# A hybrid diffusion step on one core: the low half of the attention scores with 16-bit operands

## The chip, the cores and the metric

One core of a Trainium2 chip. The metric is the time in microseconds (us) of one execution on the device. TensorE (PE in the profile) multiplies, VectorE (DVE), ScalarE (ACT) and GpSimd (POOL) do the rest, and all DMAs are issued by SyncE (SP).

## What is computed

Two layers over 256 context tokens (the prompt) and 2048 latent tokens (the samples), width 1024. A layer normalises and modulates its input, projects it to 2816 columns, runs attention (8 query heads, 2 key and value heads of 64), a short convolution and a pooling side by side, and projects back. The part that matters here:

```python
q = _rmsnorm(q.reshape(B, n, N_HEADS, HEAD_DIM), q_g)
k = _rmsnorm(k.reshape(B, n, N_KV_HEADS, HEAD_DIM), k_g)
...
s = jnp.einsum('bqkgd,btkd->bkgqt', qblk, k).astype(jnp.float32) * scale
p = jax.nn.softmax(s, axis=-1)
return jnp.einsum('bkgqt,btkd->bqkgd', p.astype(v.dtype), v)
```

The samples attend to 2048 rotated keys of their own and 256 cached ones, the prompt to its own 256.

## The kernel before

[...] To keep accuracy, an operand x is split into a high part h (x rounded to F32R) and a low part l = x - h, and a product is made of several: h*h, l*h and h*l.

**Two phases per layer.** Phase A (`phase_a`) projects: for each 256 columns of the input weights it multiplies all blocks of tokens (L473 to L475, L631 to L633; about 48 products to a unit), splits what it has, transposes q and k to head-major form and stores everything in scratch DRAM. A unit of q (`q_unit`, L531) leaves its result in one of five PSUM buffers; ACT copies it out (L487), DVE and POOL rotate it, and some units later `post` (L540) transposes it on PE (L544), copies the high part on ACT (L550), subtracts on DVE (L551) and hands two halves of each to `store`. Stores are kept back by one hook and then issued on SP, in order (`stores`, L171). The tiles of this work come from a ring of nine buffers, `w2`. `put_k` (L572) does the same for k.

Phase B (`phase_b`) is attention and the output projection. A unit is one head with 512 queries: 9 steps of 256 keys each, 32 units for the samples in a layer and 4 short ones for the prompt. `load_q1` (L1076) fills T1 with q's high and low part in the two halves of the partitions, KH holds k's high part twice, and so one product of 128 rows gives (qh + ql)*kh. `load_q2` (L1083) fills T2: 64 rows of qh and a 65th row, the shift. KL holds k's low part in 64 rows and ones in the 65th. A step (`qk`, L1151) makes for each of two key tiles

```python
nc.tensor.matmul(out=ps[:, i, :], lhsT=u.KH[u.g][:, kt], rhs=u.T1, start=True, stop=False)
nc.tensor.matmul(out=ps[:, i, :], lhsT=u.KL[u.g][0:65, kt], rhs=u.T2, start=False, stop=True)
```

The shift is minus the maximum over the keys plus a constant, so that the exponential stays in range. It is found ahead of the unit by products of their own (`max_pieces`, L1116 and L1123) with a DVE maximum after each (L1117, L1125), spread by `max_a` and `max_b` (L1143), whose last instruction writes it to T2's 65th row on ACT (L1146). After `qk` ACT takes the exponential twice, as F32 (L1165) and as F32R (L1167), POOL subtracts the two into a 16-bit low part (L180), DVE sums (L1187), and `pv` multiplies by v: the F32R part with V (L1201), and the 16-bit part with VH, a 16-bit copy of v's high half, in two column halves side by side (L1208). `round_v` (L1039) makes VH on ACT (L1041). The output projection of the block before is laid between the steps (L1328 to L1330).

The order of PE's work is written out by hand: a loop over steps calls pieces of the maximum, `qk`, `pv` three steps behind, and the output projection, at places fixed by the table `PR`. `load_kv` (L1026) loads k and v of one group; the tiles are made by `kv_tiles` (L1008). At the end of phase B `half` (L1415) loads output weights into tiles that k and v no longer need.

Of the kernel before, what the change touches and what calls it, by code (L numbers as in the profile page):

```python
# [9 lines left out]
F32 = mybir.dt.float32  # L10
# [13 lines left out]
NP = 256  # L24
# [15 lines left out]
V_SCALE = 0.0625  # L40

# [54 lines left out]
def hybrid_step(ctx: ExitStack, tc: tile.TileContext, A, O):  # L96
# [24 lines left out]
    qL = [scratch(f"qL{p}", [128, NS], F32) for p in range(4)]  # L121
    qHp = [scratch(f"qHp{p}", [128, NP], F32) for p in range(4)]
    qLp = [scratch(f"qLp{p}", [128, NP], F32) for p in range(4)]
    kH = scratch("kH", [128, NS + NC], F32)
    kL = scratch("kL", [128, NS + NC], F32)
    kHp = scratch("kHp", [128, NP], F32)
    kLp = scratch("kLp", [128, NP], F32)
# [39 lines left out]
    def store(out, in_):  # L167

        late[1].append((out, in_.bitcast(F32)))
# [18 lines left out]
    def setup(tp, ptr):  # L188
# [13 lines left out]
        nc.vector.memset(lift, P_LOG2 * float(np.log(2.0)) * 8.0)  # L202
# [63 lines left out]
    def phase_a(l, xs_src, xp_src, nxt):  # L266


        with ExitStack() as st, ExitStack() as left:
# [261 lines left out]
            def q_unit(w, b, pair, c):  # L531
# [8 lines left out]
                def post(pair, q):  # L540
# [10 lines left out]
                    nc.vector.tensor_tensor(out=lv, in0=tr, in1=hv, op=ALU.subtract)  # L551
                    t0 = b.t0 + pair * 256
                    for hp in range(2):
                        dh, dl = (qHp, qLp) if b.prompt else (qH, qL)
                        store(dh[2 * c + hp][:, t0:t0 + 256], hv[:, hp, :])
                        store(dl[2 * c + hp][:, t0:t0 + 256], lv[:, hp, :])
# [15 lines left out]
            def put_k(k, dh, dl):  # L572
# [4 lines left out]
                lo = w1("kl", F32R)  # L577
                nc.scalar.copy(out=h[:, 0:256], in_=tr)
                nc.vector.tensor_tensor(out=lo[:, 0:256], in0=tr, in1=h[:, 0:256], op=ALU.subtract)
                store(dh, h[:, 0:256])  # L580
                store(dl, lo[:, 0:256])
# [415 lines left out]
    def phase_b(l, xs_src, xp_src, xs_dst, xp_dst, nxt):  # L997
# [3 lines left out]
        with ExitStack() as st, ExitStack() as left:  # L1001
# [6 lines left out]
            def kv_tiles(prompt):  # L1008
                if prompt:
                    t = wk.tile([128, 4, 512], F32R, tag="cl", name="kvp", bufs=1)  # L1010
                    vh = wk.tile([128, 2, 2, 64], F16, tag="VHp", name="VHp", bufs=1)
                    for g in range(2):
                        for a, v in zip(kvs[True], (t[:, g, 0:256], t[:, g, 256:512],
# [6 lines left out]
                for a, t in zip(kvs[False], (p.tile([128, n], F32R, tag=f"KH{g}", name="KH"),  # L1020
                                             p.tile([65, n], F32R, tag=f"KL{g}", name="KL"),
                                             p.tile([128, n // 128, 128], F32R, tag=f"V{g}", name="V"),
                                             p.tile([128, n // 128, 64], F16, tag=f"VH{g}", name="VH"))):
                    a.append(t)

            def load_kv(prompt, g, first=True, second=True):  # L1026
# [7 lines left out]
                if second:  # L1034
                    load(KL[g][0:64, 0:n], sl[r, :])
                    nc.vector.tensor_copy(out=KL[g][64:65, 0:n], in_=ones1[64:65, 0:1].to_broadcast([1, n]))
# [46 lines left out]
            def load_q2(u):  # L1083
                sh = qHp if u.prompt else qH
                u.T2 = lk.tile([65, 512], F32R, tag="T2", name="T2", bufs=3)
                for r, ts, c in q_parts(u):
                    load(u.T2[0:64, c], sh[u.pair][r, ts])
# [625 lines left out]
```

## Time and profile before

| | us |
|---|---|
| median of 3 runs | 3377.59 |
| lowest, highest | 3371.95, 3385.19 |
| the profiled execution | 3372.27 |
| its span, first to last instruction | 3370.4 |
| PE busy | 3185.3 |
| DVE, POOL, ACT busy | 2442.1, 2136.2, 1833.3 |

The mean granted clock of TensorE is 0.98 of full speed. The first layer's phase A lasts to about 700 us, its phase B to 1690, the second layer's phases to 2345 and 3370. In the profile, L12 is line 12 of the kernel. Matmul records overlap, and their ends are modelled: the time that one of a row of them takes is read from start to start. PEld is the loading of weights, which runs beside PE.

### The profile page before, as it was taken

The page shows a single profiled execution, that of the slowest core. Times are in us where ns is not written, and L with a number is a line of the kernel's source. Part 1 is how long each engine was busy: PE and PEld are TensorE (multiplying, and loading weights), DVE is VectorE, ACT ScalarE, POOL GpSimd, SP SyncE. Part 2 cuts the span into 40 slices and gives each one's busy share as a digit, 9 for nine tenths or more (in the row PEclk, how much of TensorE's full clock was granted, in tenths as well). Part 3 has the DMA queues.
Part 4 walks back from the last instruction along what each step waited for, and adds up shares of the span by engine and source line. Part 5 has one row for each costly group of instructions (what it writes and reads, how often), then busy time and mean ns, then how long its engine had stood idle before and what let it go on. Part 6 is the DMA issues. An engine that isn't in the chain of part 4 may idle for free. (4 is left out here: it accounts for less than half of the span.)

```text
span 3370.4 us, 48172 instructions
## 1 busy us (share of the span) xinstructions
PE 3185.3 (95%) x17818; PEld 2517.4 (75%) x17818; DVE 2442.1 (72%) x3860; ACT 1833.3 (54%) x2618; POOL 2136.2 (63%) x1192
## 2 busy tenths in 40 slices
PE   6899999988999999999999999999899999999998
PEld 5888788765677777777789787987567676776777
DVE  5645575368888888888568546735888988998886
ACT  3222332248777777777543323323877677776773
POOL 3324352248888898888644345422888888888884
PEclk9999999999999999999999999999999999999999
DMA  7256635441241323232643564435123424233245
GB/s 240 72 157 204 218 125 167 135 113 34 82 147 51 101 75 93 59 101 83 203 147 98 172 197 145 128 100 128 51 66 104 133 62 126 67 110 105 74 142 197
DMA packets 367010, 405.26 MB, mean 120 GB/s; under 512 B 20788, under 2 KB 314680, under 8 KB 366008
## 3 DMA queue, kind: packets, MB, share of 16 engines
q1 hardware_dynamic: 366776, 402.18, 38.6%
q8 instruction: 142, 2.33, 0.3%
q14 instruction: 92, 0.75, 0.1%
HBM read 284.12 MB, written 117.98 MB: 119 GB/s over the span
## 5 line engine op out<-in xcount | busy, mean ns | idle before, releaser
L180 POOL TENSOR_TENSOR pl<-P,ph 128x1024 f16<-128x1024 f32 (+2 forms) x594 | 1407.6, 2379 | 328.8 <-ACT ph L1167 305.5
L1165 ACT ACTIVATE P<-st 128x1024 f32<-128x1024 f32 x576 | 635.9, 1104 | 436.7 <-PE st L1156 426.4
L1117 DVE TENSOR_REDUCE mr<-mx 128x1 f32<-128x512 f32 x1024 | 693.7, 684 | 232.5 <-PE mx L1116 230.2
L1187 DVE TENSOR_REDUCE Z<-P 128x152 f32<-128x912 f32 (+2 forms) x576 | 695.8, 1208 | 7.0 <-ACT P L1165 6.0
L1167 ACT ACTIVATE ph<-st 128x1024 fp32r<-128x1024 f32 x584 | 591.0, 1012 | 0.0
L631 PE MATMUL rest<-xh,wh 128*128 128x512 f32 (+1 forms) x1280 | 486.1, 380 | 0.3 <-ACT wh L424 0.3
L1116 PE MATMUL mx<-KH,T 128*128 128x512 f32 x1024 | 451.1, 441 | 37.1 <-DVE mr L1117 30.9
L633 PE MATMUL rest<-xh,wl 128*128 128x512 f32 (+1 forms) x1280 | 476.1, 372 | 5.2 <-DVE wl L426 3.4
L632 PE MATMUL rest<-xl,wh 128*128 128x512 f32 (+1 forms) x1280 | 476.5, 372 | 0.9 <-POOL xl L180 0.9
L1155 PE MATMUL st<-T,KH 128*128 128x512 f32 x1152 | 462.5, 402 | 1.4 <-ACT ph L1167 1.4
L1156 PE MATMUL st<-T,KL 65*128 65x512 f32 x1152 | 462.8, 402 | 0.0
L1201 PE MATMUL pv<-ph,V 128*128 128x512 f32 x1152 | 373.7, 406 | 10.1 <-DVE o L1220 10.1
L1116 PEld LDWEIGHTS mx<-KH,T 128*128 128x128 f32 x1024 | 196.4, 192 | 196.2 <-DVE mr L1117 92.8
L633 PEld LDWEIGHTS rest<-xh,wl 128*128 128x128 f32 x1280 | 243.7, 190 | 48.8 <-DVE wl L426 4.0
L426 POOL TENSOR_TENSOR wl<-wf,wh 128x512 fp32r<-128x512 f32 x88 | 123.8, 1407 | 244.3 <-ACT wh L424 229.0
L631 PEld LDWEIGHTS rest<-xh,wh 128*128 128x128 f32 x1280 | 244.3, 191 | 45.7 <-issue 7.1
L632 PEld LDWEIGHTS rest<-xl,wh 128*128 128x128 f32 x1280 | 244.3, 191 | 38.5 <-POOL xl L180 1.2
L1156 PEld LDWEIGHTS st<-T,KL 65*128 65x128 f32 x1152 | 220.9, 192 | 48.0
L1155 PEld LDWEIGHTS st<-T,KH 128*128 128x128 f32 x1152 | 221.2, 192 | 39.8 <-issue 4.2
L474 PE MATMUL qkv<-wl,xh 128*128 128x256 f32 x864 | 246.1, 285 | 4.1 <-DVE wl L426 2.9
L473 PE MATMUL qkv<-wh,xh 128*128 128x256 f32 x864 | 249.7, 289 | 0.0
L475 PE MATMUL qkv<-wh,xl 128*128 128x256 f32 x864 | 245.6, 284 | 0.0
(230 smaller groups left out, 5816.6 us busy)
## 6 DMA issues: line engine op xcount, KB each, us to landing
wo<-woH SPq DMA_DIRECT2D x68, 512.0 KB
wo<-woL SPq DMA_DIRECT2D x68, 512.0 KB
wf<-in_w_in SPq DMA_DIRECT2D x50, 512.0 KB
wa<-in_w_ada SPq DMA_DIRECT2D x24, 1024.0 KB
wf<-in_w_in SPq DMA_DIRECT2D x19, 1024.0 KB
woH<-wgh SPq DMA_DIRECT2D x64, 256.0 KB
woL<-wgl SPq DMA_DIRECT2D x64, 256.0 KB
T<-qH SPq DMA_DIRECT2D x128, 128.0 KB
```

What stands on the lines that cost most here:

```text
L180: nc.gpsimd.tensor_tensor(out=out, in0=a, in1=b, op=op)
L631: nc.tensor.matmul(out=ps[:, 0:b.n], lhsT=wh[:, k, ms], rhs=b.h[:, k, :], start=(k == 0), stop=False)
L632: nc.tensor.matmul(out=ps[:, 0:b.n], lhsT=wh[:, k, ms], rhs=b.l[:, k, :], start=False, stop=False)
L633: nc.tensor.matmul(out=ps[:, 0:b.n], lhsT=wl[:, k, ms], rhs=b.h[:, k, :], start=False, stop=(k == KD - 1))
L1116: nc.tensor.matmul(out=ps, lhsT=u.T1[:, q * 128:(q + 1) * 128], rhs=u.KH[u.g][:, c * 512:(c + 1) * 512])
L1117: nc.vector.reduce_max(out=mr[:, q, c:c + 1], in_=ps, axis=AX.X)
L1155: nc.tensor.matmul(out=ps[:, i, :], lhsT=u.KH[u.g][:, kt], rhs=u.T1, start=True, stop=False)
L1156: nc.tensor.matmul(out=ps[:, i, :], lhsT=u.KL[u.g][0:65, kt], rhs=u.T2, start=False, stop=True)
L1165: nc.scalar.activation(out=P, in_=ps, func=AF.Exp, scale=0.125)
L1167: nc.scalar.activation(out=ph, in_=ps, func=AF.Exp, scale=0.125)
L1187: nc.vector.tensor_reduce(out=z[:, c], in_=u.P[grp][:, 0:ns, c, :].rearrange("p s n t -> p n s t"), axis=AX.XY, op=ALU.add)
L1201: nc.tensor.matmul(out=u.po, lhsT=u.V[u.g][:, 2 * j + i, :], rhs=ph[:, i, :], start=(j == 0 and i == 0), stop=False)
```

## The change

T2 becomes a 16-bit float tile and is loaded from a new scratch copy of q, `qB`, in 16 bits; `post` makes this copy with one more ACT instruction and stores it. KL becomes 16-bit from `put_k` on: the subtraction writes 16 bits, the scratch tensor and its loads halve. Since the shift doesn't fit the format's steps as it is, it is stored divided by 256 (`M_SCALE`; ACT's scale and the constant `lift`), and KL's row of ones becomes a row of 256, written by a memset. KL and VH of a group become two parts of one tile, `L0` or `L1`, and the tile that takes over KL1's place at the end takes L1's.

```diff
--- before.py
+++ after.py
@@ -38,6 +38,7 @@
       'n2': 4, 'fh': 0, 'tpos': 0, 'ze': 0, 'ds': 1, 'zb': 3, 'dl': 2, 'm3': 1000, 'hk': 2, 'hc': 2,
       'fd': 12, 'n1': 9, 'h0': 22, 'h1': 16, 'h2': 10, 'fl': 2, 'dc': 256, 'el': 5, 'mapos': 1}
 V_SCALE = 0.0625
+M_SCALE = 256.0
 
 
 C_Q, C_K, C_V, C_ZA = 0, 512, 640, 768
@@ -119,12 +120,14 @@
 
     qH = [scratch(f"qH{p}", [128, NS], F32) for p in range(4)]
     qL = [scratch(f"qL{p}", [128, NS], F32) for p in range(4)]
+    qB = [scratch(f"qB{p}", [128, NS], F16) for p in range(4)]
     qHp = [scratch(f"qHp{p}", [128, NP], F32) for p in range(4)]
     qLp = [scratch(f"qLp{p}", [128, NP], F32) for p in range(4)]
+    qBp = [scratch(f"qBp{p}", [128, NP], F16) for p in range(4)]
     kH = scratch("kH", [128, NS + NC], F32)
-    kL = scratch("kL", [128, NS + NC], F32)
+    kL = scratch("kL", [128, NS + NC], F16)
     kHp = scratch("kHp", [128, NP], F32)
-    kLp = scratch("kLp", [128, NP], F32)
+    kLp = scratch("kLp", [128, NP], F16)
     vS = scratch("vS", [128, 18, 2, 128], F32)
     vSp = scratch("vSp", [128, 2, 2, 128], F32)
     zS = [scratch(f"zS{p}", [128, NS], F32) for p in range(4)]
@@ -166,7 +169,7 @@
 
     def store(out, in_):
 
-        late[1].append((out, in_.bitcast(F32)))
+        late[1].append((out, in_ if in_.dtype == F16 else in_.bitcast(F32)))
 
     def stores():
         for out, in_ in late[0]:
@@ -199,7 +202,7 @@
         nc.vector.memset(ones1, 1.0)
         nc.vector.memset(vones, V_SCALE)
         nc.vector.memset(vones_h, V_SCALE)
-        nc.vector.memset(lift, P_LOG2 * float(np.log(2.0)) * 8.0)
+        nc.vector.memset(lift, P_LOG2 * float(np.log(2.0)) * 8.0 / M_SCALE)
         nc.vector.memset(sT, 0.0)
         nc.vector.tensor_copy(out=ones_r, in_=ones1[:, 0:1].to_broadcast([128, 128]))
         pr = ptr.tile([128, 100], F32, tag="tr", name="pr")
@@ -549,9 +552,12 @@
                     lv = lo.rearrange("p (a n) -> p a n", a=2)
                     nc.scalar.copy(out=hv, in_=tr)
                     nc.vector.tensor_tensor(out=lv, in0=tr, in1=hv, op=ALU.subtract)
+                    qb = w2("qb").bitcast(F16)[:, 0:512].rearrange("p (a n) -> p a n", a=2)
+                    nc.scalar.copy(out=qb, in_=tr)
                     t0 = b.t0 + pair * 256
                     for hp in range(2):
-                        dh, dl = (qHp, qLp) if b.prompt else (qH, qL)
+                        dh, dl, db = (qHp, qLp, qBp) if b.prompt else (qH, qL, qB)
+                        store(db[2 * c + hp][:, t0:t0 + 256], qb[:, hp, :])
                         store(dh[2 * c + hp][:, t0:t0 + 256], hv[:, hp, :])
                         store(dl[2 * c + hp][:, t0:t0 + 256], lv[:, hp, :])
 
@@ -574,11 +580,11 @@
                 for i in range(2):
                     nc.tensor.transpose(tr[:, i * 128:(i + 1) * 128], k[:, i * 128:(i + 1) * 128], ident)
                 h = w1("kh", F32R)
-                lo = w1("kl", F32R)
+                lo = w1("kl").bitcast(F16)[:, 0:256]
                 nc.scalar.copy(out=h[:, 0:256], in_=tr)
-                nc.vector.tensor_tensor(out=lo[:, 0:256], in0=tr, in1=h[:, 0:256], op=ALU.subtract)
+                nc.vector.tensor_tensor(out=lo, in0=tr, in1=h[:, 0:256], op=ALU.subtract)
                 store(dh, h[:, 0:256])
-                store(dl, lo[:, 0:256])
+                store(dl, lo)
 
             def kv_unit(w, b, pair):
                 ps = qkv_mm(w, b, pair)
@@ -1010,17 +1016,17 @@
                     t = wk.tile([128, 4, 512], F32R, tag="cl", name="kvp", bufs=1)
                     vh = wk.tile([128, 2, 2, 64], F16, tag="VHp", name="VHp", bufs=1)
                     for g in range(2):
-                        for a, v in zip(kvs[True], (t[:, g, 0:256], t[:, g, 256:512],
+                        for a, v in zip(kvs[True], (t[:, g, 0:256], t[0:65, g, 256:384].bitcast(F16),
                                                     t[:, 2 + g, 0:256].rearrange("p (t e) -> p t e", e=128), vh[:, g])):
                             a.append(v)
                     return
                 n = NS + NC
                 g = len(kvs[False][0])
                 p = kvp if g else lk
-                for a, t in zip(kvs[False], (p.tile([128, n], F32R, tag=f"KH{g}", name="KH"),
-                                             p.tile([65, n], F32R, tag=f"KL{g}", name="KL"),
+                low = p.tile([128, n + n // 2], F16, tag=f"L{g}", name="L")
+                for a, t in zip(kvs[False], (p.tile([128, n], F32R, tag=f"KH{g}", name="KH"), low[0:65, 0:n],
                                              p.tile([128, n // 128, 128], F32R, tag=f"V{g}", name="V"),
-                                             p.tile([128, n // 128, 64], F16, tag=f"VH{g}", name="VH"))):
+                                             low[:, n:].rearrange("p (t e) -> p t e", e=64))):
                     a.append(t)
 
             def load_kv(prompt, g, first=True, second=True):
@@ -1032,8 +1038,8 @@
                     for i in range(2):
                         load(KH[g][64 * i:64 * i + 64, 0:n], sh[r, :])
                 if second:
-                    load(KL[g][0:64, 0:n], sl[r, :])
-                    nc.vector.tensor_copy(out=KL[g][64:65, 0:n], in_=ones1[64:65, 0:1].to_broadcast([1, n]))
+                    nc.sync.dma_start(out=KL[g][0:64, 0:n], in_=sl[r, :])
+                    nc.vector.memset(KL[g][64:65, 0:n], M_SCALE)
                     load(V[g], sv[:, :, g, :])
 
             def round_v(prompt, g):
@@ -1081,10 +1087,10 @@
                     load(u.T1[u.lo, c], sl[u.pair][r, ts])
 
             def load_q2(u):
-                sh = qHp if u.prompt else qH
-                u.T2 = lk.tile([65, 512], F32R, tag="T2", name="T2", bufs=3)
+                sb = qBp if u.prompt else qB
+                u.T2 = lk.tile([65, 512], F16, tag="T2", name="T2", bufs=3)
                 for r, ts, c in q_parts(u):
-                    load(u.T2[0:64, c], sh[u.pair][r, ts])
+                    nc.sync.dma_start(out=u.T2[0:64, c], in_=sb[u.pair][r, ts])
 
             def load_z(u):
                 z = wk.tile([128, 512], F32, tag="zs", name="zs", bufs=2)
@@ -1143,7 +1149,8 @@
             def max_b(u):
                 ps = borrow["ps"]() if borrow else pmx.tile([128, 512], F32, tag="mx", name="mxb")
                 nc.tensor.matmul(out=ps, lhsT=ones_r, rhs=u.dg)
-                nc.scalar.activation(out=u.T2[64:65, :], in_=ps[64:65, :], func=AF.Identity, bias=lift[64:65, :])
+                nc.scalar.activation(out=u.T2[64:65, :], in_=ps[64:65, :], func=AF.Identity, bias=lift[64:65, :],
+                                     scale=1.0 / M_SCALE)
 
 
             GRP = 3
@@ -1413,7 +1420,7 @@
                         state["ss"] = sm.tile([128, 4, 4], F32, tag="oss", name="oss", bufs=1)
 
                 def half(i):
-                    load_w(i // 2, i % 2, kvp.tile([128, KD, 256], F32R, tag=("KH1", "KL1", "V1")[i], name="wt"), 0)
+                    load_w(i // 2, i % 2, kvp.tile([128, KD, 256], F32R, tag=("KH1", "L1", "V1")[i], name="wt"), 0)
 
                 def later():
                     load_w(2, 1, wk.tile([128, KD, 256], F32R, tag="P", name="wt", bufs=2), 0)
```

## Rows read from the trace of the kernel before

**Rows 1.** Busy time of each engine in five stretches (start:end, length, then engines).

```profile
core 0: us, PE busy (x) PEld busy (x) DVE busy (x) ACT busy (x) POOL busy (x), PEclk, DMA share, GB/s
0.00:700.00 700.00, 648.15 (x3932) 548.52 (x3933) 388.65 (x808) 203.23 (x375) 243.96 (x207) 0.97 0.52 163
700.00:1690.00 990.00, 948.31 (x5046) 704.10 (x5045) 800.30 (x1078) 701.93 (x878) 815.24 (x385) 0.98 0.32 96
1690.00:2345.00 655.00, 626.23 (x3712) 551.25 (x3711) 384.95 (x738) 208.13 (x382) 253.91 (x209) 0.99 0.43 136
2345.00:3290.00 945.00, 897.03 (x4647) 654.06 (x4645) 820.75 (x1114) 696.80 (x947) 791.66 (x365) 0.97 0.32 96
```

**Rows 2.** The page's chain of work that ended last, shares of the span.

```profile
PE 28%; DVE 7%; DMA 2%; ACT 2%; issue 1%; POOL 1%; SPq 0%; POOLq 0%; ACTq 0%; DVEq 0%
PE mx L1116 3%; PE pv L1201 3%; PE st L1155 3%; PE st L1156 3%; PE pv L1208 2%; PE rest L633 2%; PE rest L631 2%; PE rest L632 2%; DVE mr L1117 2%; DVE Z L1187 2%; PE op L1328 1%; PE op L1329 1%; PE op L1330 1%; DMA wo<-woL 1%; PE lc L1235 1%
```

**Rows 3.** The same chain within 2345 to 3290 us, by line.

```profile
by line: PE mx L1116 11.7%; PE pv L1201 10.6%; PE st L1156 9.8%; PE st L1155 9.8%; PE pv L1208 6.5%; DVE mr L1117 6.2%; DVE Z L1187 5.4%; PE op L1328 4.6%; PE op L1329 4.5%; PE op L1330 4.4%; DMA wo<-woL 3.0%; issue 2.6%; PE lc L1235 2.5%; 
```

**Rows 4.** PE in order of time, 1009.4 to 1011.8 us: start, length, line, tiles, count.

```profile
1009.41 0.63 PE L1201 MATMUL pv<-ph,V 128*128 128x512 f32 x2
1009.98 0.62 PE L1208 MATMUL pv<-pl,VH 128*64 128x512 f16 x4
1010.53 0.50 PE L1116 MATMUL mx<-KH,T 128*128 128x512 f32 x1
1010.86 0.40 PE L1155 MATMUL st<-T,KH 128*128 128x512 f32 x1
1011.10 0.39 PE L1156 MATMUL st<-T,KL 65*128 65x512 f32 x1
1011.33 0.40 PE L1155 MATMUL st<-T,KH 128*128 128x512 f32 x1
1011.56 0.40 PE L1156 MATMUL st<-T,KL 65*128 65x512 f32 x1
1011.80 0.40 PE L1116 MATMUL mx<-KH,T 128*128 128x512 f32 x1
```

**Rows 5.** All instructions of line L1156: duration ns min/median/max, first and last start.

```profile
L1156 PE MATMUL st<-T,KL x1152: 389/399/632, 712.6 to 3305.2; 65*128 65x512 f32 x192
...
L1156 PE MATMUL st<-T,kvp x16: 393/400/628, 743.4 to 2464.8; 65*128 65x512 f32 x16
```

**Rows 6.** Durations of L1208 (1010.2 to 1010.5 us) and of L1156 (1005 to 1030 us).

```profile
L1208 PE MATMUL pv<-pl,VH x4: 379/391/403, 1010.0 to 1010.2; 128*64 128x512 f16 x4
...
L1156 PE MATMUL st<-T,KL x18: 394/396/403, 1004.6 to 1028.8; 65*128 65x512 f32 x18
```

**Rows 7.** PE in order of time around a column-tiled 32-bit product, first projection stage.

```profile
218.40 0.39 PE L631 MATMUL rest<-xh,wh 128*128 128x512 f32 x1
218.63 0.39 PE L632 MATMUL rest<-xl,wh 128*128 128x512 f32 x1
218.86 0.39 PE L633 MATMUL rest<-xh,wl 128*128 128x512 f32 x1
219.17 1.07 PE L228 MATMUL aps<-wa,sT 128*32 128x256 f32 x16
220.18 0.50 PE L631 MATMUL rest<-xh,wh 128*128 128x512 f32 x1
```

**Rows 8.** Waits, whole span: engine, line, released by, us in total, times, longest.

```profile
ACT P L1165 <- PE st L1156: 426.4, 387, 5.4
...
DVE mr L1117 <- PE mx L1116: 230.2, 343, 4.6
...
PEld mx L1116 <- DVE mr L1117: 92.8, 186, 3.3
...
PE mx L1116 <- DVE mr L1117: 30.9, 45, 3.0
...
ACT raw L487 <- DMA qH<-qh: 14.3, 3, 6.1
```

**Rows 9.** Instructions on the tile qh: SP stores, ACT copy, DVE subtraction.

```profile
L173 SPq DMA_DIRECT2D qH<-qh x64: 319/423/3204, 106.8 to 2170.4; - x64
L550 ACT CAST qh<-trq x36: 565/568/592, 104.9 to 2168.2; 128x512 fp32r<-128x512 f32 x36
L551 DVE TENSOR_TENSOR ql<-trq,qh x36: 675/684/693, 105.6 to 2169.4; 128x512 fp32r<-128x512 f32 x36
```

**Rows 10.** Busy time of each engine in stretches of the projection stages.

```profile
480.00:600.00 120.00, 119.04 (x778) 103.91 (x778) 70.78 (x183) 35.34 (x66) 38.27 (x33) 0.99 0.47 141
1790.00:1850.00 60.00, 59.23 (x490) 58.69 (x490) 47.24 (x135) 19.31 (x39) 22.45 (x21) 1.00 0.43 135
```

**Rows 11.** Groups of the constant and shift rows, and DMA issues with KB each.

```profile
L1036 DVE CAST KL<-ones 1x2304 fp32r<-1x2304 f32 x4 | 7.8, 1959 | 6.5 <-DMA mL<-ml 6.4
...
L1146 ACT ACTIVATE T<-mxb,lift 1x512 fp32r<-1x512 f32 x70 | 47.5, 679 | 2.8 <-PE mxb L1145 1.1
...
T<-qH SPq DMA_DIRECT2D x128, 128.0 KB
...
KL<-kL SPq DMA_DIRECT2D x4, 576.0 KB
```

## Prediction

> **What bounds the kernel now.** Read the stages first [rows 1]. The two attention stages (700 to 1690 and 2345 to 3290 us) take 1935 us. In them PE is busy 96% and 95% of the time; the next engines are DVE (81%, 87%) and POOL (82%, 84%). In the two projection stages PE is busy 93% and 96% and ACT only 29% to 32%. A busy PE is not PE at its peak, since matmuls overlap, so the chain of work that ended last is read next [rows 2]: it reaches back over 41% of the span, and PE holds 28 of those 41 points, DVE 7. In the second attention stage alone, the line to be changed (L1156, the second score product) is 9.8% of the window, as much as its partner L1155 [rows 3]. So the chain runs through the changed instruction, though not at all times.
>
> Then one step of the loop, in order of time [rows 4]. From 1010.86 to 1011.80 us four score products start 0.23 to 0.24 us apart, with nothing between: a 32-bit product of 512 columns occupies PE for 0.94 / 4 = 0.235 us. Everything below hangs on that spacing. The weight load of each product begins as its predecessor starts and is over before the predecessor is, so a shorter load buys nothing.
>
> **The change part by part.**
>
> *The second score product with 16-bit operands.* There are 1152 + 16 = 1168 of them [rows 5]. The kernel has 16-bit products already: the low part of PV, L1208, column-tiled in pairs. Its records fall into two lengths [rows 6]: 403 ns for the first pair of a group, which carries the exposed weight load, and 379 ns for the second. The 32-bit products of the same stretch have 394 to 403, median 396. That is 17 ns shorter, but ends are modelled, so I check it by starts. The group of four begins at 1009.98 and lasts 0.62 us, so its last pair starts at 1009.98 + 0.62 - 0.38 = 1010.22; the next product starts at 1010.53, 0.31 later [rows 4]. This contains the change of tiling, whose price a purely 32-bit place shows: L633 to the column-tiled L228 is 219.17 - 218.86 = 0.31, against 0.23 from one L631 to L633 product to the next [rows 7], so 0.08 to 0.09 us. What is left for the 16-bit product is 0.22 us, against 0.235. I take 17 ns: 1168 x 17 ns = **19.9 us less on PE**. Bounds: nothing (lengths and starts are uncertain by about as much), and, if the following 32-bit product gained as much, 40 us.
>
> *How much of this reaches the end.* In the second layer 584 of the products occupy 584 x 0.235 = 137 us, and the chain holds 9.8% of 945 = 93 us of them [rows 3], 68%. The rest lies beside DVE: PE's loads of the maximum product waited 92.8 us for DVE's maxima, and PE itself 30.9 us [rows 8]; there a faster PE only waits longer. 19.9 x 0.68 = **13.5 us**. If all landed, 20 us.
>
> *Changing type between neighbours.* Each 16-bit product now stands between 32-bit ones, so PE changes type 2336 times. The trace shows such a change only together with one of tiling. It costs the same there (the second L1201 starts at 1009.41 + 0.63 - 0.40 = 1009.64, L1208 at 1009.98: 0.34 less 0.235, so 0.1) as the change of tiling between 32-bit products [rows 4, 7]. I therefore take 0 for the type. The upper bound is a whole visit to L1208: from 1009.64 to the product at 1010.86 is 1.22 us for four products' worth of time, 0.94, so 0.28 us. The changed product keeps 65 rows and 128 columns, so it is not tiled.
>
> *The copy of q.* Each of 36 head transposes gets one more ACT copy, priced like the existing one at 568 ns, 36 x 0.57 = 20.5 us, and two more stores (72 SP issues of about 0.42 us, 30 us of SP) [rows 9]. All of it lies in the projection stages. In the two stretches chosen there PE is busy 99%, ACT 29% and 32% [rows 10]: PE hides it. Without that cover it is 20.5 us, and 36 x 0.68 = 24.6 more if the ACT copy has to follow DVE's subtraction out of the same bank: 45 us. The third buffer per transpose turns the ring of nine work buffers faster; waits on it exist (ACT raw for the store of qh: 14.3 us in 3 times [rows 8]) and may double, but five PSUM buffers stand between ACT and PE. I take 1 us. What is queued behind the copy on ACT (raw copies, weight casts) moves by half a microsecond. On SP the new stores go ahead of those of qh and ql; their waits were there before.
>
> *Small edits.* The 64 loads of T2 for the sample rows halve from 128 KB, the four of KL from 576 KB [rows 11]; the attention stages have DMA at 0.32 [rows 1], so nothing. The constant row of KL becomes a memset in place of a cast that cost 1.96 us four times [rows 11]: between 0 and -8 us of DVE, 0 taken. The ACT write of the shift row keeps its shape, 679 ns [rows 11]; the scale rides along. KL and VH share one tile; VH's four casts come where they came before.
>
> **Sum.** 0 - 13.5 + 1 = -12.5 us. The profiled execution took 3372.3 us (span 3370.4), 5.3 below the median of the runs shown, so against the median 3377.6 I forecast **3365 us**, 0.4% less. A measurement of this kernel tells about 0.5%, 17 us, from no change.
>
> **Rivals.**
>
> 1. *More lands than the chain says.* Where PE waits for DVE, DVE had often waited for PE (230.2 us for the maximum product, ACT 426.4 us for the score product [rows 8]), so a faster PE pulls both forward. 20 us and up to the 40 of the upper bound: about 3357, at best 3340. For it: no other engine is above 87% busy. Against it: the waits above.
>
> 2. *The width buys nothing.* If the 0.235 us is the price of 512 columns whatever their type, PE gains 0, and time is 3378 + 1, say 3379. The recorded 379 against 396 speaks against it; that these ends are modelled, and that the starts leave 0.22 with an uncertainty of 0.01, speaks for it. [...]
>
> 3. *Slower, by the change of type.* The place is PE between L1155 and L1156, twice for each product. If a change of type makes PE empty itself, it costs up to 0.28 us for each visit: 1168 x 0.28 = 327 us, of which the chain's 68% is 222: 3600, with half the price 3489. It turns into a loss as soon as a visit costs over 17 ns. For it: every 16-bit group of the trace has a gap on both sides. Against it: the same gap stands between 32-bit products where the tiling changes [rows 7].
>
> 4. *Slower, by the projection stages.* The extra copy and the ring make ACT late in freeing PSUM, and the 45 us above come onto the path: 3378 - 13 + 45 = 3410. It would need ACT to fall behind by five units of qkv products; ACT has two thirds of its time free.
>
> That the program would not do what it says (the product still run as 32-bit) is not a live case, since both operands are declared 16-bit and loaded so.
>
> **How the numbers follow.** Forecast (13.5 us land, give or take 6): 0.50, split evenly on both sides of the 17 us, since a median moves by some microseconds too. Rival 1: 0.16, faster. Rival 2: 0.19, of which 0.18 the same and 0.01 slower. Rival 3: 0.10, slower. Rival 4: 0.05, slower. Faster 0.25 + 0.16 = 0.41; same 0.25 + 0.18 = 0.43; slower 0.01 + 0.10 + 0.05 = 0.16. The range reaches down to rival 1's best case and up past rival 2 by the scatter of the runs (8 us from the median to the highest) and a few microseconds of the ring: 3340 to 3392. Rivals 3 and 4 (0.15) are left out, and a little of the edges. The forecast's own range is 3352 to 3376.
>
> **What the profile of after would show.** Right: L1156 with 16-bit forms, records near 380 ns and 0.215 to 0.22 us to the next start, L1155 unchanged at 0.235; four score products in 0.90 to 0.91 us instead of 0.94; PE's wait for DVE's maxima some microseconds up; the projection stages as long as before to within 2 us, with 36 more ACT copies. Wrong: a gap on PE before or after L1156 (rival 3); unchanged 0.235 (rival 2); a projection stage longer by over 10 us, with ACT raw or the store of the copy as releaser (rival 4); attention stages shorter by 20 us or more together (rival 1).

## The result and the profile after

| us | before | after |
|---|---|---|
| median | 3375.47 | 3399.94 |
| lowest, highest | 3370.47, 3385.19 | 3394.21, 3403.39 |
| span of the profiled execution | 3370.4 | 3399.2 |

The ratio is 1.0068, with a 95% interval from 1.0052 to 1.0083: the change makes the kernel slower by 24 us, where 12 us faster was forecast, and the time lies above the range.

To find the stage that pays, cut both executions at the same work and not at the same times: at the first and the last KH product (the line of [rows 4] that starts a step) of each layer. First the busy time of each engine in the four stretches of the kernel after (start:end, length, then engines).

```profile
core 0: us, PE busy (x) PEld busy (x) DVE busy (x) ACT busy (x) POOL busy (x), PEclk, DMA share, GB/s
0.00:719.30 719.30, 663.50 (x3985) 560.55 (x3986) 390.71 (x817) 214.63 (x397) 243.18 (x207) 0.97 0.51 161
719.30:1657.50 938.20, 902.72 (x4744) 567.16 (x4743) 780.28 (x1054) 690.68 (x860) 804.19 (x377) 0.98 0.29 86
1657.50:2356.90 699.40, 662.53 (x3936) 585.66 (x3935) 384.44 (x747) 218.11 (x402) 257.38 (x216) 0.97 0.45 143
2356.90:3333.90 977.00, 921.43 (x4745) 577.98 (x4743) 834.18 (x1137) 715.08 (x972) 807.01 (x377) 0.97 0.31 94
```

The same cuts in the kernel before.

```profile
0.00:712.40 712.40, 660.55 (x3986) 558.55 (x3987) 394.94 (x818) 205.20 (x380) 243.96 (x207) 0.97 0.51 161
712.40:1655.40 943.00, 904.47 (x4745) 664.45 (x4744) 782.13 (x1054) 691.21 (x860) 805.93 (x378) 0.98 0.30 89
1655.40:2334.70 679.30, 651.53 (x3934) 576.88 (x3933) 392.74 (x747) 208.46 (x383) 258.44 (x215) 0.99 0.46 145
2334.70:3305.00 970.30, 916.77 (x4744) 667.82 (x4743) 835.47 (x1138) 715.42 (x972) 808.17 (x378) 0.98 0.32 97
```

The number of PE instructions is the same to within two, so the lengths can be compared. The projection stages grew by 6.9 and 20.1 us, 27 together. The attention stages, where the gain should be, went by -4.8 and +6.7. (That makes 28.8 us between the two executions; the profiled one of before lies 3 us under the median above, that of after 1 us over its own.) In the second projection stage PE's idle time (length less busy) rose from 27.8 to 36.9 us, and its busy time rose by 11 us for the same products. The granted clock beside it fell from 0.99 to 0.97, which over 680 us is 13.6 us by these rounded figures, an estimate. So the loss there has two halves: PE waits longer, and it runs slower.

Who waits for whom stands in the waits of the kernel after (engine, line, released by, us in total, times, longest).

```profile
ACT P L1172 <- PE st L1163: 431.9, 385, 5.1
PEld L1163 <- issue: 306.2, 1163, 0.5
POOL wl L429 <- ACT wh L427: 299.6, 57, 18.6
DVE mr L1123 <- PE mx L1122: 227.4, 339, 4.5
...
ACT qb L556 <- DVE ql L554: 132.1, 31, 10.0
...
ACT raw L490 <- PE qkv L478: 44.8, 11, 7.2
```

The rows of attention (ACT P, DVE mr) answer to [rows 8] and hardly moved. Two lines are new. ACT's copy of q waits 132.1 us for DVE's subtraction, 31 times out of 36. And the weight load of the changed product starts late 1163 times out of 1168, by 0.26 us each time, "issue": nothing that the profile shows holds it. Two old lines moved; in the waits of the kernel before they read

```profile
POOL wl L426 <- ACT wh L424: 229.0, 47, 19.2
...
ACT raw L487 <- PE qkv L475: 112.1, 26, 9.0
```

POOL waits 299.6 us for ACT's weight casts, 229.0 before. And ACT waits for PE's qkv products only 44.8 us in 11 times, 112.1 us in 26 times before: that line was ACT's slack (the time by which it is ahead of its supplier), and more than half of it is spent.

Here is one of the 31. ACT in order of time in the kernel after (in brackets the idle time before, and what ended it).

```profile
1822.92 0.58 ACT L553 CAST qh<-trq 128x512 fp32r<-128x512 f32 x1 [1.85 <-POOL ra L183]
1831.19 0.58 ACT L556 CAST qb<-trq 128x512 f16<-128x512 f32 x1 [7.69 <-DVE ql L554]
1831.67 0.59 ACT L490 COPY raw<-qkv 128x512 f32<-128x512 f32 x1
...
1838.03 0.58 ACT L556 CAST qb<-trq 128x512 f16<-128x512 f32 x1 [4.57 <-DVE ql L554]
```

DVE in the same stretch.

```profile
1822.43 3.36 DVE L516 TENSOR_TENSOR sq<-raw,trig 128x128 f32<-128x128 f32 x4
1825.72 0.16 DVE L156 TENSOR_SCALAR nt_v<-hs 128x16 f32<-128x16 f32 x1
...
1829.26 1.29 DVE L525 TENSOR_TENSOR ra<-ra,nt_y 128x512 f32<-128x512 f32 x2
1830.47 0.68 DVE L554 TENSOR_TENSOR ql<-trq,qh 128x512 fp32r<-128x512 f32 x1
```

ACT is ready for the copy at 1823.5. DVE has the subtraction in its queue behind a rotation and a whole chain of small normalisation steps and gets to it at 1830.47. Both only read the transposed q, the one PSUM tile `trq`. The copy starts at 1831.19, when the subtraction is over (1830.47 and 0.68 us), and for 7.69 us the raw copies and weight casts behind it on ACT stand still. So one reader waits here for the other, 31 times; what makes it wait the trace doesn't show. Three of PE's own waits in the second projection stage, kernel after, show where this reaches it:

```profile
PE qkv L476 <- ACT wh L427: 3.2, 1, 3.2
...
PE trq L547 <- ACT qb L556: 1.7, 1, 1.7
...
PE rest L637 <- ACT wh L427: 1.7, 1, 1.7
```

In the same stage of the kernel before, the first two aren't there and the third is 0.3 us. They are a weight cast that stands on ACT behind the copy, and a PSUM buffer of the transposes that the copy still reads. In neither kernel does a qkv product wait for ACT's raw copy: their five PSUM buffers never ran out. And over the stretch that the prediction had picked as the proof of its cover [rows 10], kernel after:

```profile
1790.00:1850.00 60.00, 54.82 (x457) 54.21 (x456) 40.87 (x126) 19.65 (x38) 18.70 (x16) 1.00 0.43 133
```

PE is busy 54.82 us of 60, with 457 products, where it had 59.23 and 490 (the kernel after began this stage 2 us later). ACT is busy 19.65 us, as before (19.31): its share never showed the danger.

The second new line, on PE. A step of the kernel after, PE in order of time.

```profile
1018.82 0.39 PE L1162 MATMUL st<-T,KH 128*128 128x512 f32 x1
1019.05 0.39 PE L1163 MATMUL st<-T,L 65*128 65x512 f16 x1
1019.09 0.59 PE L1162 MATMUL st<-T,KH 128*128 128x512 f32 x1
1019.52 0.39 PE L1163 MATMUL st<-T,L 65*128 65x512 f16 x1
```

The weight loads of the same step.

```profile
1018.59 0.19 PEld L1162 LDWEIGHTS st<-T,KH 128*128 128x128 f32 x1
1019.04 0.10 PEld L1163 LDWEIGHTS <-L 65*128 65x128 f16 x1 [0.26 <-issue]
1019.05 0.20 PEld L1162 LDWEIGHTS st<-T,KH 128*128 128x128 f32 x1
1019.51 0.10 PEld L1163 LDWEIGHTS <-L 65*128 65x128 f16 x1 [0.26 <-issue]
```

Don't read single gaps here: a 32-bit product behind a 16-bit one has its start recorded 0.04 us after it, and a record of 0.59 us. Read pairs: from one L1163 to the next it is 0.47 us here, as for a pair of 32-bit products; the median of all such pairs at full clock is 0.461 us, against 0.469 in the kernel before. The load of the 16-bit weights takes half the time (0.10 against 0.19 us), but it begins 0.22 us after the 32-bit product before it has started, about when that has streamed, and not as it starts.

### The profile page after: what moved, and what is told of

Read it like the earlier page. It is cut to its first block, busy times and chain, and to the rows that moved or that the text cites. A ratio compares the mean times of both kernels' runs of the same rounds, so it can differ in the third digit from the quotient of the medians.

```text
span 3399.2 us, 48325 instructions
## 1 busy us (share of the span) xinstructions
PE 3203.6 (94%) x17818; PEld 2342.1 (69%) x17818; DVE 2426.7 (71%) x3860; ACT 1851.6 (54%) x2654; POOL 2131.6 (63%) x1192
## 5 line engine op out<-in xcount | busy, mean ns | idle before, releaser
L1122 PE MATMUL mx<-KH,T 128*128 128x512 f32 x1024 | 528.4, 517 | 36.5 <-DVE mr L1123 28.5
L1162 PE MATMUL st<-T,KH 128*128 128x512 f32 x1152 | 505.1, 497 | 1.5 <-ACT ph L1174 1.5
L1163 PE MATMUL st<-T,L 65*128 65x512 f16 x1152 | 458.5, 398 | 0.0
L1208 PE MATMUL pv<-ph,V 128*128 128x512 f32 x1152 | 386.1, 417 | 10.2 <-DVE o L1227 10.2
L1163 PEld LDWEIGHTS <-L 65*128 65x128 f16 x1152 | 113.5, 99 | 300.8 <-issue 300.1
L429 POOL TENSOR_TENSOR wl<-wf,wh 128x512 fp32r<-128x512 f32 x88 | 121.7, 1384 | 299.6 <-ACT wh L427 299.6
L1162 PEld LDWEIGHTS st<-T,KH 128*128 128x128 f32 x1152 | 229.9, 200 | 13.4 <-issue 4.2
```

The costliest lines, as they stand in the source:

```text
L1122: nc.tensor.matmul(out=ps, lhsT=u.T1[:, q * 128:(q + 1) * 128], rhs=u.KH[u.g][:, c * 512:(c + 1) * 512])
L1208: nc.tensor.matmul(out=u.po, lhsT=u.V[u.g][:, 2 * j + i, :], rhs=ph[:, i, :], start=(j == 0 and i == 0), stop=False)
```

## The experiments

Three theories for the loss: **Theory 1**, ACT's wait for DVE in the projection stages; **Theory 2**, the change of type on PE; **Theory 3**, the ring of work buffers and the 72 more stores. Later, on the size of the gain: **Theory A**, a 16-bit weight load isn't taken ahead behind a 32-bit product but is behind a 16-bit one; **Theory B**, it is never taken ahead. "Stage" below is a stretch between the cuts of the section above; each ratio is to runs of the kernel before on the same chip.

**The copy ahead of the subtraction** (the kernel after, two lines moved)

```diff
                     nc.scalar.copy(out=hv, in_=tr)
+                    qb = w2("qb").bitcast(F16)[:, 0:512].rearrange("p (a n) -> p a n", a=2)
+                    nc.scalar.copy(out=qb, in_=tr)
                     nc.vector.tensor_tensor(out=lv, in0=tr, in1=hv, op=ALU.subtract)
-                    qb = w2("qb").bitcast(F16)[:, 0:512].rearrange("p (a n) -> p a n", a=2)
-                    nc.scalar.copy(out=qb, in_=tr)
```

> The changed kernel with the 16-bit copy of q issued on ACT ahead of DVE's subtraction out of the same bank, so that ACT no longer waits for DVE there. Theory 1 (the loss is ACT's wait for DVE's subtraction, 132.1 us in 31 times, which holds up the projection stages): back to the time of before or a little under it, 3365 to 3380, both projection stages within 4 us of before. Theory 2 (the loss is the change of type on PE in the attention stages): still 3395 to 3405. Theory 3 (the loss is the third work buffer and the added stores): still 3395 to 3405.

3384.45 us, ratio 1.0022 (1.0007 to 1.0038): some 15 of the 24 us are gone by the order of two instructions. The time lies in nobody's range, 4 us above that of Theory 1 and 10 under those of the others. For what the copy waited (DVE sq and DMA qB) and who waited for it (the last two rows), in this kernel:

```profile
L555 ACT CAST qb<-trq x36: 586/586/609, 104.3 to 2177.0; 128x512 f16<-128x512 f32 x36
...
  DVE sq L516: 19.4, 9
  DMA qB<-qb: 7.6, 5
...
  DVE ql L556: 18.9, 12
  ACT raw L490: 16.6, 5
```

The wait has turned round: DVE waits for ACT, 18.9 us in 12 times. What the copy and the raw copy still wait for here are buffers of the ring. ACT has more than half of the lost slack back, and the second projection stage is 685.1 us long instead of 699.4:

```profile
ACT raw L490 <- PE qkv L478: 84.6, 20, 8.3
```

**The copy made from the high part in SBUF** (the kernel after; the copy no longer reads `trq`)

```diff
-                    nc.scalar.copy(out=qb, in_=tr)
+                    nc.scalar.copy(out=qb, in_=hv)
```

> The changed kernel with the 16-bit copy made from the high half in SBUF in place of the transposes in PSUM; order, buffers and stores stay. Theory 1: 3365 to 3380, no wait of the copy for DVE. Theory 2: 3395 to 3405. Theory 3: 3395 to 3405, since the ring and the stores are the same.

3385.23 us, ratio 1.0022 (1.0004 to 1.0039), the same as by moving it, and again some 5 us above Theory 1's range. The copy takes 619 ns in place of 585 and waits for the subtraction no more: the trace has no such wait in its 36 times. Two different ways of avoiding the wait for DVE, which both keep the ring and the stores, give back the same 15 us; Theories 2 and 3, by which both would have stayed at 3395 or more, don't explain these 15.

**The copy alone** (the kernel before, 32-bit products and all, with the copy and its stores, which nobody reads)

```diff
                     nc.vector.tensor_tensor(out=lv, in0=tr, in1=hv, op=ALU.subtract)
+                    qb = w2("qb").bitcast(F16)[:, 0:512].rearrange("p (a n) -> p a n", a=2)
+                    nc.scalar.copy(out=qb, in_=tr)
...
+                        store(db[2 * c + hp][:, t0:t0 + 256], qb[:, hp, :])
```

> The kernel before with the copy of q and its stores added, as the change has them; nothing reads them and the score products stay 32-bit. Theory 1: 3395 to 3405, the projection stages 20 to 27 us longer, the attention stages as before. Theory 2: 3373 to 3380. Theory 3: 3395 to 3405.

3403.29 us, ratio 1.0075 (1.0057 to 1.0093), 27.6 us. That is all of the loss, with no 16-bit product in the kernel, which rules out Theory 2 as its cause. The projection stages are 11.0 and 17.1 us longer. Its waits show the same two lines as those of the kernel after:

```profile
ACT qb L555 <- DVE ql L553: 133.2, 32, 10.2
...
ACT raw L489 <- PE qkv L477: 45.0, 11, 7.2
```

**The copy alone, ahead of the subtraction** (the two lines of the kernel above in the order of the first experiment)

> The kernel before with the copy of q and its stores added, unread, the copy issued ahead of DVE's subtraction. Theory 1 (ACT's wait for DVE was the loss): 3374 to 3382, the projection stages within 6 us of before. Theory 3 (ring and stores): 3395 to 3405.

3384.70 us, ratio 1.0026 (1.0007 to 1.0045). So the order is worth 18.6 us without the products too, and 9 us stay: the time is 3 us above Theory 1's range and 10 under that of Theory 3.

**The copy alone, ahead, without its stores**

```diff
-                        store(db[2 * c + hp][:, t0:t0 + 256], qb[:, hp, :])
```

> copy_alone_first without the stores: the kernel before with ACT's copy of q ahead of DVE's subtraction, into a work buffer that nobody reads or stores. It asks what carries the 9 us that copy_alone_first still lost (1.0026). If the copy itself does (half a microsecond of ACT, DVE's subtraction later by as much): 1.0020 to 1.0030, 3382 to 3385. If the 72 stores do (their place in SP's queue, the buffer held until they land): 0.9995 to 1.0010, 3374 to 3379.

3381.08 us, ratio 1.0016 (1.0000 to 1.0033), between the two answers. It doesn't tell them apart.

**The product alone** (the kernel after without the copy and its stores; T2 is loaded from the bytes of qH)

```diff
-                    qb = w2("qb").bitcast(F16)[:, 0:512].rearrange("p (a n) -> p a n", a=2)
-                    nc.scalar.copy(out=qb, in_=tr)
...
-                    nc.sync.dma_start(out=u.T2[0:64, c], in_=sb[u.pair][r, ts])
+                    nc.sync.dma_start(out=u.T2[0:64, c], in_=sb[u.pair].bitcast(F16)[r, ts])
```

> The changed kernel without the copy and its stores: T2 is filled with as many bytes out of the scratch of q's high half, so the low score term is not the right one. Theories 1 and 3: 3366 to 3378, attention stages 0 to 10 us shorter together. Theory 2: 3395 to 3405.

3380.43 us, ratio 1.0019 (1.0002 to 1.0035), above the range of Theories 1 and 3 and far under that of Theory 2. The product brings nothing; if anything it costs. Counted in the trace from the first score product of a step to the first product behind the four and the maximum, at full clock, the median of some 290 steps is 1158 ns, in the kernel before 1174. That is 8 ns for each changed product, not 17.

**Both low products after both high ones** (the first experiment's kernel)

```diff
-                for i in range(2):
-                    kt = slice((2 * j + i) * 128, (2 * j + i + 1) * 128)
+                kts = [slice((2 * j + i) * 128, (2 * j + i + 1) * 128) for i in range(2)]
+                for i, kt in enumerate(kts):
                     nc.tensor.matmul(out=ps[:, i, :], lhsT=u.KH[u.g][:, kt], rhs=u.T1, start=True, stop=False)
+                for i, kt in enumerate(kts):
                     nc.tensor.matmul(out=ps[:, i, :], lhsT=u.KL[u.g][0:65, kt], rhs=u.T2, start=False, stop=True)
```

> The changed kernel with the copy ahead of the subtraction, and in each step the two 32-bit score products first and the two 16-bit ones behind them. Theory A (a 16-bit weight load isn't taken ahead behind a 32-bit product, but is behind a 16-bit one; each exposed load eats the shorter stream): the second 16-bit product starts 0.216 us after the first, PE saves some 25 ns for each of 584 steps, 10 us of it land: 3370 to 3380. Theory B (a 16-bit load is never taken ahead): spacing 0.24 for both, time as with the copy ahead, 3380 to 3390.

3381.00 us, ratio 1.0007 (0.9992 to 1.0022). The instructions of the low product's line in this kernel:

```profile
L1164 PEld LDWEIGHTS <-L x1152: 96/100/148, 715.9 to 3313.4; 65*128 65x128 f16 x192
...
  issue: 164.1, 584
```

584 late loads in place of 1163: exactly the first of each two. The second, behind a 16-bit product, is taken ahead, as Theory A has it. The step is 1149 ns, 9 less. The time doesn't decide: it lies 1 us above Theory A's range, in that of Theory B, and its interval overlaps that of the first experiment. The second 16-bit product starts 0.228 us behind the first, not the 0.216 of Theory A.

**The same order in the kernel before**

> The kernel before with the same order of the four score products, all 32-bit: the control for the order alone. Both theories: as before, 3370 to 3381.

3376.40 us, ratio 1.0007 (0.9990 to 1.0024): the order alone does nothing to the time. Its steps are 1168 ns, 6 less than in the kernel before, so of the 9 ns above only 3 stand clear of what the order does by itself.

**All score products with 16-bit operands** (the first experiment's kernel; KH is filled from k's low part and T1 from the copy of q twice, so that KH, KL, T1 and T2 are all 16-bit and the scores are not the right ones)

```diff
-                for a, t in zip(kvs[False], (p.tile([128, n], F32R, tag=f"KH{g}", name="KH"), low[0:65, 0:n],
+                for a, t in zip(kvs[False], (p.tile([128, n], F16, tag=f"KH{g}", name="KH"), low[0:65, 0:n],
...
-                u.T1 = lk.tile([128, 512], F32R, tag="T1", name="T1", bufs=4)
+                u.T1 = lk.tile([128, 512], F16, tag="T1", name="T1", bufs=4)
```

> The changed kernel with the copy ahead, and with the first score product and the products of the maximum 16-bit too; KH and T1 are filled with the 16-bit low half of k and the 16-bit q, so the scores are not the right ones. Theory A: score and maximum products start 0.216 to 0.22 us apart, with no idle time of PE's loads ahead of them; about 1024 + 1152 + 1152 products by 17 ns, 57 us less on PE, two thirds of it landing: 3325 to 3350. Theory B: spacing 0.24, time 3375 to 3395.

3328.74 us, ratio 0.9857 (0.9829 to 0.9884), 47 us less. PE in order of time:

```profile
1021.35 0.38 PE L1162 MATMUL st<-T,KH 128*128 128x512 f16 x1
1021.57 0.38 PE L1163 MATMUL st<-T,L 65*128 65x512 f16 x1
1021.79 0.38 PE L1162 MATMUL st<-T,KH 128*128 128x512 f16 x1
1022.01 0.38 PE L1163 MATMUL st<-T,L 65*128 65x512 f16 x1
```

and the low product's line:

```profile
L1163 PE MATMUL st<-T,L x1152: 379/380/634, 714.9 to 3260.0; 65*128 65x512 f16 x192
...
  issue: 12.0, 38
```

The products stand 0.22 us apart, the loads are late 38 times. A 16-bit product among its like does save the 17 ns: the 1152 low, 1152 high and 1024 maximum products that became 16-bit, at 17 ns, are 57 us, of which 47 came off the time, 83%, the copy's cost included. It came where the products are: in the profiled execution the attention stages are 35.6 and 18.7 us shorter. This run also loads fewer bytes, whose share in the gain it doesn't tell apart.

**No copy, low products grouped** (the product alone, in the new order: the best that the idea can give here)

> No copy of q, no stores of one (T2 is loaded from the bytes of qH as 16-bit numbers, so the low score term is left out), and within a step the two products with KH first, then the two with KL. The best that the 16-bit product can do here without a third 16-bit operand. Theory A (a 16-bit weight load is not taken ahead behind a 32-bit product, is behind a 16-bit one): steps of 1149 ns as in low_grouped against 1158 in product_alone, 584 steps x 9 ns = 5 us less than product_alone's 3380, so 3373 to 3377, no different from before. If what low_grouped lost was the copy alone and the grouped steps land fully (25 ns x 584 = 15 us against before): 3362 to 3367. If half-rate spells of the clock take it back: 3378 to 3382.

3371.78 us, ratio 0.9984 (0.9966 to 1.0002). Steps of 1150 ns, as Theory A had them. The time is some 5 us less by the ratio, just short of telling it from no change, and lies between two of the ranges given, 1 us under Theory A's.

**The copy on POOL, from SBUF, low products grouped**

```diff
-                    nc.scalar.copy(out=qb, in_=tr)
+                    nc.gpsimd.tensor_copy(out=qb, in_=hv)
```

> low_grouped, with the copy of q made by POOL from qh in SBUF in place of ACT from PSUM. Theory 1 (what is left of the copy's loss is ACT's half microsecond ahead of DVE's subtraction): projection stages as before to within 3 us, 3372 to 3377. Rival (the ring of work buffers and the 72 stores carry it): projection stages 5 to 9 us longer, as in copy_before_sub and low_grouped, 3379 to 3383. Rival (POOL's copy delays the rotation of the next q, which needs POOL): over 3385.

3389.84 us, ratio 1.0039 (1.0024 to 1.0054), slower than with ACT's copy ahead of the subtraction. The third expectation had the number, by a delay of the rotation on POOL. The trace shows another wait beside it, the ring's, which holds ACT up; the run doesn't tell the two apart:

```profile
ACT raw L490 <- DMA qB<-qb: 38.2, 8, 6.2
```

**The same with buffers of its own** (two for the copy, the ring cut from nine to eight)

```diff
-                    qb = w2("qb").bitcast(F16)[:, 0:512].rearrange("p (a n) -> p a n", a=2)
+                    qb = tp.tile([128, 2, 256], F16, tag="qb", name="qb", bufs=2)
...
-                return tp.tile([128, 512], dt, tag="w2", name=name, bufs=9)
+                return tp.tile([128, 512], dt, tag="w2", name=name, bufs=8)
```

> grouped_pool_copy, with two buffers of its own for the copy and the ring of work buffers cut from nine to eight. If the copy's cost lies in the ring, the time moves against grouped_pool_copy: shorter by 3 to 6 us if a copy waiting for its store holds the ring, longer by 2 to 10 us if the ring of nine was just enough for the others. If the ring does not matter: the same to within 2 us.

3386.07 us, ratio 1.0034 (1.0020 to 1.0048). The wait of ACT raw for the copy's store is gone from the profile. The time is less by 3.8 us by the medians and by 1.7 by the ratios, the same to within the intervals, so that it decides between none of the three expectations: the wait may have cost little, or the eight buffers as much as it.

## Why the prediction was wrong

**What bounds the kernel: right.** PE fills all stages (busy 92 to 96% of each in the kernel after), and the chain that ended last within the second layer's attention, kernel after, has the lines and nearly the shares of [rows 3]:

```profile
by line: PE mx L1122 11.7%; PE pv L1208 10.5%; PE st L1163 10.2%; PE st L1162 10.1%; PE pv L1215 6.5%; PE op L1335 4.9%; DVE mr L1123 4.9%; PE op L1336 4.8%; PE op L1337 4.6%; DVE Z L1194 4.4%; DMA wo<-woL 2.7%; PE lc L1242 2.7%; issue 2.4%
```

**The failed step: "The copy of q", "I take 1 us".** It measured 27.6 us alone, and it is the loss; 18.6 of them go with the order of the copy and the subtraction. The prediction wrote the wait down as a bound, "36 x 0.68 = 24.6 more if the ACT copy has to follow DVE's subtraction out of the same bank: 45 us", and then dropped it for reasons that the trace after refutes. First, "PE hides it": PE was 99% busy there and hid nothing, since its own supply came from the engine that was delayed; its products fell from 490 to 457 in that very stretch. Second, "ACT has two thirds of its time free": the raw copy behind the waiting copy stood still with it, for the 7.69 us of the trace above, and what counted was not ACT's share of busy time but how early it was, which the line that the prediction left unread showed: 112.1 us of waiting for qkv products, of which 67 were used up. Third, "five PSUM buffers stand between ACT and PE": they do, and no qkv product waited for one, but the delay went round them, by the weight casts and by the transposes' own buffer. And the wait was priced too low: not DVE's 0.68 us but 132.1 / 31 = 4.3 us, because DVE's subtraction stands behind a normalisation chain. The prediction asked what is queued behind the copy on ACT and answered "half a microsecond"; it didn't ask what is queued ahead of the subtraction on DVE, which the copy has to wait out. Rival 4, forecast 3410 with a chance of 0.05, had the stage and nearly the size, but not the path: PSUM was not freed late, and its "five units" weren't needed.

How 132 us of waiting on ACT come to 27 on the whole: most of it only eats slack; PE's idle time in the second projection stage rose by 9 us. The other half there is the clock. In the kernel before the granted clock was 0.5 in two spells, 10 us together, in this stage; after it is in six, 38 us. In the 10 us ahead of each of the six PE had been idle for 1.6 to 3.4 us, ahead of the two for 5.0 and 3.7; the stage's average for 10 us is 0.5 after and 0.4 before. Half of the 27 us more is 13.6 us, of which PE's busy time shows 11. With the copy alone the spells there are 24 us, PE's idle time 37.4 us and the stage 17.1 us longer, so the idle time comes back alike and the spells don't. Over all its runs the copy alone had a mean clock of 0.976 against 0.978; by the relation given below, an estimate, that goes with some 5 of its 27.6 us. The other kernels with the copy have 20 to 31 us of such spells there, those without it 10 to 17. That the stalls bring the spells is argued from this; no run forces a spell by itself.

**The failed term: 17 ns for each product.** A 16-bit product saves 17 ns (0.235 to 0.218 with all scores 16-bit: six spacings of score products at 1018 and 1021 us of that run take 1.31 us), so rival 2, the width buys nothing, is refuted. But "Changing type between neighbours ... I therefore take 0" hid the other half, and so did "The weight load of each product begins as its predecessor starts", which was read from 32-bit products and stops being true for the changed ones. At the change to 16 bits the weight load isn't taken ahead, 1163 times out of 1168; at the change back L1162's are no later than in the kernel before (12 waits, 4.2 us, in both); and of the 17 ns 8 are left: 9.3 us in place of 19.9. Rival 3 had the place, at some 9 ns a product and not 280. The comparison in the prediction, L1208, has just this late load in its first product of each group ("403 ns for the first pair of a group, which carries the exposed weight load"); it was put down to tiling. The waits of the kernel before had it too:

```profile
PEld L1208 <- issue: 158.5, 404, 2.0
```

There the tiling changes with the type, so that line alone couldn't tell the two apart; but it is a price, and it was taken as 0. Every changed product is the first of its group. The load itself is shorter, 97 against 189 ns (the medians of L1163 after and L1156 before). It was taken ahead for 32 bits behind 32 (L1156 in the kernel before: none late), for 16 behind 16 (the second of each two with the low products grouped, 584) and for 32 behind 16 (L1162 in the kernel after, but for the 12 waits); for 16 behind 32 it wasn't, 1163 times. Why, the trace doesn't show.

**"68% lands": of 9.3 us, nothing was seen.** Grouped and without the copy, with 25 ns less for each of 584 steps, 14.6 us, the kernel gains 5 (by the interval from 11 gained to 1 lost). In the product alone the steps are shorter by as much as the trace says, and the time is not. Its second attention stage took 979.8 us at a clock of 0.97, the kernel before 970.3 at 0.98. If that hundredth were the cause it would be 9.7 us. It isn't this execution alone: the mean granted clock of the 12 runs of the product alone is 0.974, that of the 29 runs of the kernel before on the same chip 0.978, and among those 29 a clock lower by 0.001 went with 2.0 us more. By that, an estimate, the lower clock goes with 8 us, about what the shorter steps gave (584 x 16 ns = 9.3 us). With all scores 16-bit the clock stayed at 0.978, and most of the gain came through. What lowers the clock when only the low product changes stays open. (The prediction's "about 0.5%, 17 us" as what a measurement tells was too wide: the intervals of the runs here, but for that with all scores 16-bit, are 5 to 6 us to either side.)

**Small edits, 0: nothing speaks against it.** The memset takes 1.98 us, as the cast did [rows 11]. KL and VH in one tile brought no wait that shows, and the DMA share of the attention stages fell from 0.32 to 0.31 in the second layer.

**What still costs 9 us** with the copy ahead of the subtraction is not settled: stores, ring, half a microsecond of ACT, or the clock after small stalls. The traces lean to stores and ring. Without the stores the copy waits 7.3 us in place of 30.6. And the second projection stage, cut as above, is 678.7 to 680.4 us long in the four kernels without a copy, 681.4 with the copy ahead and unstored, 683.3 to 686.9 in the five in which ACT makes and stores it without waiting for DVE's subtraction, 692 and 693 on POOL, 696.4 and 699.4 behind the subtraction. Each is one execution.

No version here that computes the right scores beats the kernel before. The best of them, with the copy ahead and the low products grouped, is no different from it (1.0007).

## What to carry to other kernels

Before adding an instruction to an engine with free time, look at what it must wait for, and at what stands ahead of that on the other engine's queue. Here, of two engines that read one PSUM tile, the second waited for the first in either order: ACT for DVE 132.1 us, 31 times, DVE for ACT 18.9 us, 12 times. In such a place try the two copies of one engine in a row and the other engine last, worth 15 to 18.6 us in this kernel. Look at how long the engine waits for its supplier, not at its share: that wait was the slack which the delay used up here, 67 of 112.1 us. Where 16-bit and 32-bit products mix, try the 16-bit ones side by side: only the first of each two had the late load (584 of 1168), though in this kernel that brought 9 ns a step and no time clear of the scatter.

## What was not expected of the hardware

- Behind a 32-bit product, the 16-bit weight loads of the kernel after started 0.26 us late, about when that product had streamed: 1163 late loads of 1168. There were 584 when the 16-bit products stood in twos, and 38 when the score and maximum products beside them were all 16-bit. A visit to 16 bits and back cost about 9 ns of the 17 when the products alternated (15 of 34 when they stood in twos, against the same order in 32 bits), an estimate from the steps of 1174, 1158, 1168 and 1149 ns. Every run has as many changes out as in, so that no time splits the price; the late loads stand at the change in.
- Score products of 512 columns stood 0.218 us from start to start with 16-bit operands (all scores 16-bit) and 0.235 us with 32-bit ones (the kernel before).
- An ACT copy of 0.58 us, 36 times, cost 27.6 us behind DVE's read of the same PSUM tile and 9 us ahead of it.
